# Joining small TensorE runs: scores and values of two head pairs together, retention's values turned, the compressed branch's first layer on four column groups

## The chip, the cores and the metric

One core of a Trainium2 chip. The time is what the device takes for one launch, in microseconds (us), on inputs of a fixed seed. The numbers are medians of several runs; a profile is one execution, recorded by the hardware profiler. Lower is better. The engines are TensorE (PE, with its weight loads shown apart as PEld), VectorE (DVE), ScalarE (ACT), GpSimd (POOL) and SyncE (SP), which issues the transfers.

## What is computed

Two transformer blocks over 256 tokens of width 1024, batch 1. The first block mixes four attention branches, each weighted by a gate of the normed input, then runs a gated feed-forward layer with a width-3 convolution. The second mixes retention with differential attention, attends to a memory of 256 tokens, and ends in another feed-forward layer. Cut to what the change touches:

```python
# first block
o_a = nsa_mixer(...)        # 4 heads of 64: compressed + selected + windowed attention, added with gates
o_b = dilated_mixer(...)    # 3 groups of 2 heads of 64, merged by a joint softmax
o_c = forgetting_mixer(...) # 4 heads (64, and 2 more columns for the decay)
o_d = mla_mixer(...)        # 4 heads (64 + 32 rotary)
merged = sum(sigmoid(h @ w_merge_gate[i]) * (o_i @ w_branch[i]))
# in nsa_mixer: 15 overlapping blocks of 32 tokens x 64, flattened to 2048
def compress(kv, w1, w2):
    blocks = (blocks + cmp_pos).reshape(b, n_cmp, 2048)
    return gelu(blocks @ w1) @ w2       # w1 2048 x 128, for keys and for values
# second block
scores = einsum('bhncd,bhnjd->bhncj', q, k) * decay        # retention, 8 heads of 64
o_ret = scores @ v
a = softmax(q0 k0) - lam * softmax(q1 k1)                  # difference, 4 heads, 2 maps of 64
o_diff = a @ v                                             # v 128 wide
```

## The kernel before

**Products.** The large matrices are streamed in panels. `W` (L479) loads a panel of fp32 weights into a `raw` slot, ACT rounds it to a shorter format into `hi`, DVE writes the remainder into `lo`; `mm3` (L492) then adds three products (high by high, high by low, low by high). `lin` (L597) does this for a panel of 512 columns and two halves of 128 tokens. The attention products work on plain fp32: one such product is two records in the trace.

**Planner.** Nothing is issued as it is written. `Plan.add` collects each operation with its operands; `Plan.trial` simulates the engines with the costs that `_Op` gives each operation, with limited slots for each class of buffer (8 PSUM banks `PS`; in SBUF 3 `raw`, 8 `hi`, 8 `lo`, 6 `k4`, 2 `g4`, 10 `k2`, 9 `k1` and others, L423), and picks by priority; a buffer is taken only if enough are free. `hurry` changes priorities where PE would wait, 120 trials are made, and the shortest is issued in its order of starts. So every change of cost or of buffers plans the whole order anew. `glue` (L160) makes all PE operations inside it one item of the plan, issued without a break. `AN.copy` and `AN.scale` go to DVE or ACT, whichever the plan finds free.

**Attention.** A head pair is worked together: `scores` (L645) issues four products, two heads by two halves of queries, glued; for 64-row heads the two heads stand on rows 0 to 63 and 64 to 127 of the array. DVE adds the bias and takes the minimum, `expo` (ACT) the exponential with its sum, `transP` (L666) transposes three 128 x 128 blocks on PE and copies them back, and `values` (L675) issues four products, glued, whose 64 held columns write partitions 0 to 63 and 64 to 127 of one bank. `attend` (L684) strings these together for one pair and one set of keys. The plain branches d and c call it twice each, branch a four times (two pairs, selected and windowed); branch b (L1165 to L1188) calls `scores` three times, then `values` three times.

**The compressed branch** (L1065 to L1121). The input is split into `hi` and `lo` pieces of 30 columns side by side (`blk`), the four panels of `w1` go through `W`, and 32 products of 256 columns, 60 or 30 columns held, are added in one bank of 60 partitions; `fold` adds the two halves and turns the result.

**Second block** (L1453 to L1499). Retention: for each of four pairs a glued run of score products, DVE multiplies by the decay, then three products per head with 128 columns of scores held and the 64 columns of a head's values moved, into two banks of 128 tokens x 512. The difference heads call `scores` once each.

Of the kernel before, what the change touches and what calls it, by code (L numbers as in the profile page):

```python
# [16 lines left out]
OP = mybir.AluOpType  # L17
# [3 lines left out]
class Plan:  # L21
# [137 lines left out]
    @contextmanager  # L159
    def glue(self):  # L160

        self.gluing = True
        yield
        self.gluing, self.glued = False, None

    def trial(self, prio):
# [29 lines left out]
        while done < len(ops):  # L196
# [15 lines left out]
            for e, hp in heaps.items():  # L212
# [3 lines left out]
                while hp:  # L216
# [5 lines left out]
                    ok = True  # L222
                    for nm in o.own:
                        if nm in place:
                            continue
                        c = self.cls[nm]
                        need = 1 if order[c][ptr[c]] == nm else 1 + (99 if o.dma else self.reserve.get(c, 99))
# [122 lines left out]
class _Op:  # L350
    def __init__(self, plan, n, eng, go, name, outs, ins, k):
# [8 lines left out]
        elif eng == "PE":  # L360
            n_ = size if name == "matmul" else 128
            if name == "transpose":
# [55 lines left out]
def emit(ctx, tc, nc, T, out, dbg):  # L418
# [226 lines left out]
    def scores(qk, bias, mn, at):  # L645

        ps = [psS([128, 384]) for _ in qk]
        ss = [sb([128, 384], "k2", name="s") for _ in qk]  # L650
        plan.hold = list(ss)
        with plan.glue():
            for tt in (1, 0):
                for p, (q, k) in zip(ps, qk):
                    PE.matmul(p[:, COLS[tt]], q[:, tt * 128:tt * 128 + 128], k[:, :128 * (tt + 1)], start=True, stop=True)
        for tt in (1, 0):
            for u, (p, s) in enumerate(zip(ps, ss)):
                c = at(tt, u)
                V.tensor_tensor_reduce(s[:, COLS[tt]], p[:, COLS[tt]], bias[u][tt], 1.0, 3e38, op0=OP.add, op1=OP.min,
                                       accum_out=mn[:, c:c + 1])  # L660
        return ss
# [13 lines left out]
    def values(po, pts, vs, first, last):  # L675

        blocks = ((0, slice(0, 256), slice(0, 256)), (1, slice(128, 256), slice(256, 384)))
        with plan.glue():
            for n, (j, c, w) in enumerate(blocks if first else blocks[::-1]):
                for u in range(2):  # L680
                    PE.matmul(po[64 * u:64 * u + 64, c], vs[u][j], pts[u][:, w], start=first and n == 0,
                              stop=last and n == 1, skip_group_check=first and last)

    def attend(po, qk, bias, vs, gain=None, first=True, last=True):  # L684

        mn, den, rec = small(4), small(4), small(4)
        ss = scores(qk, bias, mn, lambda tt, u: 2 * tt + u)
        for tt in (1, 0):
            for u in range(2):
                c = slice(2 * tt + u, 2 * tt + u + 1)  # L690
                expo(ss[u], tt, mn[:, c], den[:, c])
        V.reciprocal(rec, den)
        if gain is not None:
            for tt in range(2):
                V.tensor_mul(rec[:, 2 * tt:2 * tt + 2], rec[:, 2 * tt:2 * tt + 2], gain(tt))
        for u in range(2):
            for tt in (1, 0):
                AN.scale(ss[u][:, COLS[tt]], ss[u][:, COLS[tt]], rec[:, 2 * tt + u:2 * tt + u + 1])
        pts = [transP(s) for s in ss]
        values(po, pts, vs, first, last)  # L700
# [17 lines left out]
def mats1(E):  # L718
# [229 lines left out]
    def plain(q, k, v, kd, key):  # L948

        oT = heads(key, 2)  # L950
        for p in range(2):
            hs = (2 * p, 2 * p + 1)
            po = psS([128, 256])
            attend(po, [(q[:kd, h], k[:kd, h]) for h in hs], [(cm(0), cm(1))] * 2,
                   [[v[j][:, h, :] for j in range(2)] for h in hs])
            outT(oT, p, po)
# [36 lines left out]
    aqT = sb([128, 2, 256], "k4", name="aqT")  # L993
# [68 lines left out]

    gate(0, "d")

    posT = sb([128, 16], "sm", name="posT")  # L1065
    G.dma_start(posT, T["posT"])
    w2 = sb([128, 2, 64], "k1", name="w2")
    G.dma_start(w2, T["w2"])
    blk = sb([128, 16, 60], "k8", F32R, name="blk")
    for kv in range(2):  # L1070
        t = sb([128, 16, 15], "k1", name="blkf")
        for par in range(2):
            base = akT[par * 64:(par + 1) * 64, kv, par:par + 1]
            src = bass.AP(tensor=base.tensor, offset=base.offset, ap=[list(base.ap[0]), [2, 16], [16, 15]])
            V.tensor_add(t[par * 64:(par + 1) * 64], src,
                         posT[par * 64:(par + 1) * 64, :, None].to_broadcast([64, 16, 15]))
        hh = blk[:, :, 15 * kv:15 * kv + 15]
        S.copy(hh, t)
        V.tensor_sub(blk[:, :, 30 + 15 * kv:45 + 15 * kv], t, f(hh))
# [11 lines left out]
    hn = sb([60, 256], "k1", name="h1n")  # L1091
    V.tensor_copy(hn, hp)
    fold = sb([60, 30], "k1", name="fold")
    V.tensor_add(fold, ident[:60, :30], ident[:60, 30:60])
    ht = psS([128, 64])
    for kv in range(2):
        PE.matmul(ht[:, 32 * kv:32 * kv + 30], hn[:, 128 * kv:128 * kv + 128], fold, start=True, stop=True)
    h1 = bass.AP(tensor=ht.tensor, offset=ht.offset, ap=[list(ht.ap[0]), [47, 2], [1, 15]])
    hs = sb([128, 3, 2, 15], "k1", name="gelu")
# [5 lines left out]
    w2k = sb([128, 2, 64], "k1", name="w2k")  # L1105
    V.tensor_copy(w2k, w2[:, 0, None, :].to_broadcast([128, 2, 64]))
    hv = sb([128, 4, 32], "k1", name="hv")
    V.memset(hv, 0.0)
    V.tensor_copy(hv[:, :, :15], hs[:, 0, 1, None, :].to_broadcast([128, 4, 15]))
    kc = sb([128, 2, 16], "k1", name="kc")  # L1110
# [42 lines left out]
    for pr in range(2):  # L1153
        po = psS([128, 256])
        for b in range(2):
            attend(po, [(aqT[64 * u:64 * u + 64, pr], akT[64 * u:64 * u + 64, 2 + b]) for u in range(2)],
                   [(tb(2 * pr + u, 0), tb(2 * pr + u, 1)) for u in range(2)],
                   [[av[j][:, b * 64:(b + 1) * 64] for j in range(2)]] * 2,
                   lambda tt: gts[tt][:, 2 * pr:2 * pr + 2, 1 + b], b == 0, False)
# [6 lines left out]
    ss = [scores([(bq[64 * j:64 * j + 64, gi], bk[64 * j:64 * j + 64, gi]) for j in range(2)],  # L1166
                 [(tb(4 + 2 * gi + j, 0), tb(4 + 2 * gi + j, 1)) for j in range(2)], mn,
                 lambda tt, j: 6 * tt + 3 * j + gi) for gi in range(3)]
# [591 lines left out]
```

## Time and profile before

| | |
|---|---|
| median of 3 runs | 871.64 us (871.44 to 871.86) |
| the profiled execution | 872.01 us |
| its span, first to last instruction | 870.2 us |
| PE busy | 858.7 us (99%), 4453 records of products |
| DVE busy | 663.0 us (76%) |
| ACT busy | 479.5 us (55%) |
| granted TensorE clock, mean | 0.997 |

A product's shown length contains the way through the array, so that neighbours overlap; what a product costs in a stream is the distance from its start to the next one's. "128\*64 128x256" in a row is held rows by held columns, then the written shape. The chip time of the profiled execution is 1.8 us above its span.

### The profile page before, as it was taken

Reading aid. Unit: us, or ns where it says so; the run is one execution under the profiler, and the core shown is the slowest. Engines: PE = TensorE matmul, PEld = TensorE weight load, DVE = VectorE, ACT = ScalarE, POOL = GpSimd, SP = SyncE. Lnnn points to the kernel's source line nnn. Section 1 sums busy time; section 2 is a strip of 40 time slices with the busy share of each in tenths; the row PEclk is TensorE's granted clock in tenths of the full one; section 3 lists DMA queues with packets and bytes.
Section 4 is the critical chain, followed back from the end, with each engine's and each line's share of the span. In section 5 each row is a group of like instructions: output and inputs, shape, how many; then the busy total and the mean of one; then the engine's idle time right before and its main releaser. Section 6 shows DMA issues by size and latency. Waiting matters only on the chain.

```text
span 870.2 us, 12251 instructions
## 1 busy us (share of the span) xinstructions
PE 858.7 (99%) x4453; PEld 719.8 (83%) x4453; DVE 663.0 (76%) x1201; ACT 479.5 (55%) x810; POOL 45.3 (5%) x58
## 2 busy tenths in 40 slices
PE   8999999999999999999999999999999999999998
PEld 7789877778887888888878887888888888888886
DVE  6986766775778999898988677968775687776663
ACT  5775564764555766655654357645644545544440
POOL 2100000000001000000010111201100000000000
PEclk9999999999999999999999999999999999999999
DMA  7657745466447666666536564454643566666641
GB/s 225 207 191 217 218 148 164 160 198 213 144 148 241 195 212 211 204 195 192 193 122 198 167 194 149 143 169 145 208 131 97 187 200 216 215 182 185 198 141 49
DMA packets 45200, 156.07 MB, mean 179 GB/s; under 512 B 5142, under 2 KB 6984, under 8 KB 45012
## 3 DMA queue, kind: packets, MB, share of 16 engines
q1 hardware_dynamic: 44228, 153.09, 56.1%
q0 software_dynamic: 896, 2.19, 0.8%
q8 instruction: 35, 0.57, 0.3%
q14 instruction: 25, 0.20, 0.1%
q10 hardware_dynamic: 16, 0.00, 0.0%
HBM read 154.21 MB, written 1.06 MB: 178 GB/s over the span
## 4 chain that ended last, share of the span: by engine, by line
PE 89%; DVE 5%; issue 2%; ACT 1%; DMA 1%; POOL 1%; DVEq 0%; POOLq 0%; ACTq 0%
PE bank L102 89%; DVE k L102 2%; DVE lo L102 1%; DVE x L102 1%; POOL sm L102 1%; DMA raw<-in_fdn 1%; DMA raw<-in_fupn 1%; ACT x L102 0%; DVE sm L102 0%; ACT junk L102 0%; ACT k L102 0%; ACT hi L102 0%; ACT k L112 0%; DVEq L1756 0%; ACT sm L102 0%
## 5 line engine op out<-in xcount | busy, mean ns | idle before, releaser
L102 PE MATMUL bank<-hi,x 128*128 128x512 f32 (+3 forms) x1556 | 494.3, 392 | 2.2 <-DVE x L102 1.4
L102 DVE TENSOR_TENSOR lo<-raw,hi 128x1024 fp32r<-128x1024 f32 (+3 forms) x280 | 334.7, 1203 | 79.5 <-ACT hi L102 77.9
L102 ACT CAST hi<-raw 128x1024 fp32r<-128x1024 f32 (+3 forms) x280 | 288.7, 1036 | 140.2 <-PE bank L102 57.9
L102 PEld LDWEIGHTS bank<-hi,x 128*128 128x128 f32 (+1 forms) x1556 | 288.5, 188 | 57.6 <-ACT hi L102 2.5
L102 PE MATMUL bank<-lo,x 128*128 128x512 f32 (+3 forms) x786 | 305.7, 391 | 2.7 <-DVE lo L102 2.2
L102 PEld LDWEIGHTS bank<-lo,x 128*128 128x128 f32 (+1 forms) x786 | 146.6, 187 | 33.0 <-DVE lo L102 4.5
L102 PE MATMUL bank<-x,hi 128*128 128x512 f32 x656 | 167.9, 392 | 0.0
L102 PEld LDWEIGHTS bank<-x,hi 128*128 128x128 f32 x656 | 119.2, 189 | 21.3
L102 PEld LDWEIGHTS bank<-x,lo 128*128 128x128 f32 x656 | 89.7, 190 | 6.5
L102 PE MATMUL bank<-x,lo 128*128 128x256 f32 x656 | 91.8, 282 | 0.0
L112 ACT COPY k<-bank 128x256 f32<-128x256 f32 (+3 forms) x78 | 31.1, 409 | 56.8 <-PE bank L102 52.3
L102 POOL TENSOR_TENSOR sm<-sm,nhalf 128x1 f32<-128x1 f32 (+3 forms) x36 | 35.8, 997 | 492.8 <-DVE sm L102 492.8
L102 PE MATMUL bank<-ident,k 128*128 128x128 f32 (+3 forms) x347 | 53.3, 275 | 1.0 <-DVE k L102 0.7
L102 PEld LDWEIGHTS bank<-ident,k 128*128 128x128 f32 (+3 forms) x347 | 41.5, 138 | 13.8 <-DVE k L102 4.7
L102 DVE TENSOR_TENSOR x<-bank,x 128x512 fp32r<-128x512 f32 (+4 forms) x62 | 36.2, 606 | 20.4 <-PE bank L102 19.4
L102 PE MATMUL bank<-k,k 64*128 64x256 f32 (+12 forms) x364 | 49.9, 327 | 0.7 <-ACT k L112 0.6
L102 PEld LDWEIGHTS bank<-k,k 64*128 64x128 f32 (+4 forms) x364 | 38.7, 176 | 11.5 <-issue 4.9
L102 DVE COPY k<-bank 128x256 f32<-128x256 f32 (+7 forms) x60 | 28.1, 473 | 22.3 <-PE bank L102 22.0
L102 DVE TENSOR_TENSOR k<-k,bank 128x256 f32<-128x256 f32 (+1 forms) x78 | 32.5, 418 | 8.2 <-ACT k L112 7.5
L102 ACT ACTIVATE k<-bank,sm 128x256 f32<-128x256 f32 (+1 forms) x38 | 20.0, 554 | 28.4 <-PE bank L102 17.4
L102 DVE SCALAR_TENSOR_TENSOR k<-k,k,k 128x255 f32<-128x255 f32 x72 | 34.3, 479 | 1.5 <-ACT k L102 0.7
L102 ACT ACTIVATE k<-k,sm 128x128 f32<-128x128 f32 (+1 forms) x60 | 26.6, 446 | 7.5 <-DVE sm L102 7.4
(121 smaller groups left out, 439.4 us busy)
## 6 DMA issues: line engine op xcount, KB each, us to landing
raw<-in_wi SPq DMA_DIRECT2D x42, 512.0 KB, 4.4
raw<-in_up SPq DMA_DIRECT2D x40, 512.0 KB, 4.1
raw<-in_fup SPq DMA_DIRECT2D x36, 512.0 KB, 4.3
raw<-in_wg SPq DMA_DIRECT2D x32, 512.0 KB, 4.3
raw<-in_fdn SPq DMA_DIRECT2D x22, 512.0 KB, 4.5
raw<-in_dn SPq DMA_DIRECT2D x22, 512.0 KB, 4.6
raw<-in_xkv SPq DMA_DIRECT2D x16, 512.0 KB, 4.3
raw<-in_wo SPq DMA_DIRECT2D x8, 512.0 KB, 4.4
```

The costliest lines, as they stand in the source:

```text
L102: op = _Op(self, n, eng, lambda: getattr(target, name)(*map(self.place, a), **{x: self.place(y) for x, y in k.items()}), name, outs, ins, k)
L112: alt = _Op(self, n, e2, lambda: getattr(t2, n2)(*map(self.place, a2), **k2), n2, outs, ins, k2)
```

## The change

- `scores`, `values` and `attend` take a list of jobs. The products of all jobs in a call stand in one glued run; the steps between are as before, job by job. Branches c and d pass both head pairs, branch a the selected and the windowed attention of a pair, branch b two groups and then one to `scores`, all three to `values`. The difference heads go two by two.
- Retention's scores go two pairs a run. Its values are issued by `values`: the 64 columns of a head's values are held and up to 256 columns of scores moved, which gives the outputs turned round (head columns by tokens); a copy and two transposes for each pair bring them into the same two output banks.
- The first compressed layer takes plain fp32 weights in two `g4` slots and an unsplit input (one `k2` tile): for each of 16 steps and for keys and values one product, 15 columns held and 128 moved, on one of four groups of 32 columns. It is issued in two glued runs of 16 products. A small product with `fold` adds the groups, after four copies.
- `aqT` goes from class `k4` to `k2`; several small tiles of the compressed branch share a tile.
- The planner: a glued item costs 300 ns more; small fp32 products inside a glued item cost half (64 rows or columns) or a quarter (15 columns) of before; an item that takes several buffers needs that many free.

The core of the diff:

```diff
+        self.glued.cost += extra
...
+                        k = taken[c] = taken.get(c, 0) + 1
+                        need = k if order[c][ptr[c]] in o.own else k + (99 if o.dma else self.reserve.get(c, 99))
...
+            elif plan.gluing and m == 15:
+                self.cost = n_ / 2.4 + 2.0
+            elif plan.gluing and (m == 64 or p == 64):
+                self.cost = n_ * 2 / 2.4 + 2.0
...
+    def scores(jobs):
...
+        ps = [[psS([128, 384]) for _ in j[0]] for j in jobs]
+        ss = [[sb([128, 384], "k2", name="s") for _ in j[0]] for j in jobs]
+        plan.hold = [x for y in ss for x in y]
         with plan.glue():
+            for j, pj in zip(jobs, ps):
+                for tt in (1, 0):
+                    for p, (q, k) in zip(pj, j[0]):
+                        PE.matmul(p[:, COLS[tt]], q[:, tt * 128:tt * 128 + 128], k[:, :128 * (tt + 1)], start=True, stop=True)
+        for (qk, bias, mn, at), pj, sj in zip(jobs, ps, ss):
...
+    def values(jobs):
...
-            for n, (j, c, w) in enumerate(blocks if first else blocks[::-1]):
+            for po, pts, vs, first, last in jobs:
+                for n, (j, c, w) in enumerate(blocks if first else blocks[::-1]):
+                    for u in range(2):
+                        PE.matmul(po[64 * u:64 * u + 64, c], vs[u][j], pts[u][:, w], start=first and n == 0,
+                                  stop=last and n == 1, skip_group_check=first and last)
+
+    def attend(jobs):
...
+        mds = [(small(4), small(4)) for _ in jobs]
+        sss = scores([(j[1], j[2], md[0], lambda tt, u: 2 * tt + u) for j, md in zip(jobs, mds)])
+        vals = []
...
+            vals.append((po, [transP(s) for s in ss], vs, first, last))
+        values(vals)
...
+        attend([(pos[p], [(q[:kd, h], k[:kd, h]) for h in (2 * p, 2 * p + 1)], [(cm(0), cm(1))] * 2,
+                 [[v[j][:, h, :] for j in range(2)] for h in (2 * p, 2 * p + 1)], None, True, True) for p in range(2)])
...
-    aqT = sb([128, 2, 256], "k4", name="aqT")
+    aqT = sb([128, 2, 256], "k2", name="aqT")
...
+    blk = sb([128, 2, 16, 15], "k2", name="blk")
...
+    hp = psS([128, 128])
+    for cc in ((0, 1), (2, 3)):
+        ws = [sb([128, 1024], "g4", name="w1") for c in cc]
+        for c, w in zip(cc, ws):
+            plan.bulk = True
+            nc.sync.dma_start(w, T["w1"][c])
+            plan.bulk = False
+        with plan.glue():
+            for c, w in zip(cc, ws):
+                for i in range(4):
+                    for kv in range(2):
+                        r = 32 * (2 * (i % 2) + kv)
+                        PE.matmul(hp[r:r + 15], blk[:, kv, 4 * c + i], w[:, i * 256 + kv * 128:i * 256 + kv * 128 + 128],
+                                  start=c == 0 and i < 2, stop=c == 3 and i > 1)
...
-    hp = psS([60, 256])
-    for c in range(4):
-        hi, lo = W(T["w1"][c], 1024)
-        for i in range(4):
-            k = 4 * c + i
-            w = slice(i * 256, (i + 1) * 256)
-            if k == 15:
-                PE.matmul(hp[:30], blk[:, k, :30], lo[:, w], start=False, stop=False)
-            PE.matmul(hp, blk[:, k, :], hi[:, w], start=k == 0, stop=k == 15)
-            if k < 15:
-                PE.matmul(hp[:30], blk[:, k, :30], lo[:, w], start=False, stop=False)
...
+    for r in (0, 32, 64, 96):
+        AN.copy(hn[r:r + 15], hp[r:r + 15])
+    h1 = psS([128, 2, 15])
+    PE.matmul(h1.rearrange("p a c -> p (a c)"), hn, p1[:, 218:248], start=True, stop=True)
...
+        attend([(po, [(aqT[64 * u:64 * u + 64, pr], akT[64 * u:64 * u + 64, 2 + b]) for u in range(2)],
+                 [(tb(2 * pr + u, 0), tb(2 * pr + u, 1)) for u in range(2)],
+                 [[av[j][:, b * 64:(b + 1) * 64] for j in range(2)]] * 2,
+                 lambda tt, b=b: gts[tt][:, 2 * pr:2 * pr + 2, 1 + b], b == 0, False) for b in range(2)])
...
+    ss = scores([job(0), job(1)]) + scores([job(2)])
...
+        vals.append((po, pts, [[bv[kt][:, 2 * gi + j, :] for kt in range(2)] for j in range(2)], gi == 0, gi == 2))
+    values(vals)
...
-            PE.matmul(po[0][:, h, :], d[:, :128], rv[0][:, h, :], start=True, stop=True)
-            PE.matmul(po[1][:, h, :], d[:, 128:256], rv[0][:, h, :], start=True, stop=False)
-            PE.matmul(po[1][:, h, :], d[:, 256:], rv[1][:, h, :], start=False, stop=True)
+            for i, p in enumerate(pp):
+                for j in range(2):
+                    for u in range(2):
+                        r = slice(64 * u, 64 * u + 64)
+                        PE.matmul(ps[i][u][:, 256 * j:256 + 128 * j], rkT[r, p, 128 * j:128 * j + 128], rqT[r, p, 128 * j:],
+                                  start=True, stop=True)
...
+        pT = [psS([128, 256]) for _ in pp]
+        values([(pT[i], ds[i], [[rv[j][:, 2 * p + u, :] for j in range(2)] for u in range(2)], True, True)
+                for i, p in enumerate(pp)])
+        for i, p in enumerate(pp):
+            oT = sb([128, 256], "k1", name="rT")
+            AN.copy(oT, pT[i])
+            for tt in range(2):
+                PE.transpose(po[tt][:, 2 * p:2 * p + 2, :].rearrange("p h d -> p (h d)"), oT[:, tt * 128:tt * 128 + 128], ident)
...
+    for hp in ((0, 1), (2, 3)):
+        mds = [(small(4), small(4)) for _ in hp]
+        sss = scores([([(dqT[64 * b:64 * b + 64, h], dkT[64 * b:64 * b + 64, h]) for b in range(2)], [(cm(0), cm(1))] * 2,
+                       mds[i][0], lambda tt, b: 2 * b + tt) for i, h in enumerate(hp)])
```

## Rows read from the trace of the kernel before

**Rows 1.** The page's engine table: busy us, share of the span, instructions.
```profile
PE 858.7 (99%) x4453; PEld 719.8 (83%) x4453; DVE 663.0 (76%) x1201; ACT 479.5 (55%) x810; POOL 45.3 (5%) x58
```
**Rows 2.** Slices of 20 us: length, busy us of each engine, clock, DMA.
```profile
0.00:20.00 20.00, 16.93 (x75) 14.76 (x76) 13.84 (x50) 11.83 (x27) 4.61 (x11) 0.91 0.71 227
...
860.00:880.00 20.00, 6.26 (x28) 4.86 (x26) 2.83 (x5) 0.00 (x0) 0.00 (x0) 0.92 0.14 53
```
**Rows 3.** PE in order of time near 122 us: start, length, products, idle before.
```profile
121.92 0.39 PE L102 MATMUL bank<-hi,x 128*128 128x512 f32 x1
...
122.37 0.39 PE L102 MATMUL bank<-hi,x 128*128 128x512 f32 x1
122.69 0.92 PE L102 MATMUL bank<-k,k 64*128 64x256 f32 x8
...
123.88 0.40 PE L102 MATMUL bank<-lo,x 128*128 128x512 f32 x1
```
**Rows 4.** The same near 534 us: three calls of the difference heads.
```profile
533.66 0.62 PE L102 MATMUL bank<-hi,x 128*128 128x512 f32 x2
534.21 2.23 PE L102 MATMUL bank<-k,k 64*128 64x256 f32 x24
...
536.71 0.40 PE L102 MATMUL bank<-hi,x 128*128 128x512 f32 x1
```
**Rows 5.** The same near 136 and 148 us: one and two calls of values.
```profile
135.84 0.87 PE L102 MATMUL bank<-k,k 128*64 128x256 f32 x8
136.64 0.74 PE L102 MATMUL bank<-hi,x 128*128 128x512 f32 x2
...
147.83 1.52 PE L102 MATMUL bank<-k,k 128*64 128x256 f32 x16
149.28 0.50 PE L102 MATMUL bank<-hi,x 128*128 128x512 f32 x1
149.61 0.40 PE L102 MATMUL bank<-lo,x 128*128 128x512 f32 x1
```
**Rows 6.** The same: the first 64-row scores, and one ahead of values.
```profile
101.42 0.92 PE L102 MATMUL bank<-k,k 64*128 64x256 f32 x8
...
138.01 1.72 PE L102 MATMUL bank<-k,k 64*128 64x256 f32 x16
```
**Rows 7.** The same: the first and the last values of the first block.
```profile
49.15 1.41 PE L102 MATMUL bank<-k,k 66*128 66x128 f32 x12
...
179.22 1.52 PE L102 MATMUL bank<-k,k 128*64 128x128 f32 x16
```
**Rows 8.** PE by form, 488.3 to 490.7 us: busy us, mean ns, idle.
```profile
L102 PE MATMUL bank<-k,k 128*128 128x64 f32 x22 | 2.6, 272 | 0.0
```
**Rows 9.** PE in order of time near 543 us: transposes.
```profile
543.03 1.36 PE L102 MATMUL bank<-ident,k 128*128 128x128 f32 x11
```
**Rows 10.** The same from 154 to 161 us: the compressed branch's first layer.
```profile
154.44 0.30 PE L102 MATMUL bank<-hi,x 128*60 128x256 f32 x1 [0.82 <-DVE x L102]
...
158.11 0.75 PE L102 MATMUL bank<-hi,x 128*60 128x256 f32 x3
158.79 0.92 PE L102 MATMUL bank<-k,k 64*128 64x256 f32 x8
160.66 0.50 PE L102 MATMUL bank<-lo,x 128*128 128x512 f32 x1 [0.95 <-DVE lo L102]
```
**Rows 11.** DVE by form, 148 to 162 us.
```profile
L102 DVE TENSOR_TENSOR lo<-raw,hi 128x1024 fp32r<-128x1024 f32 x4 | 4.8, 1218 | 0.8 <-ACT hi L102 0.8
```
**Rows 12.** Slices of 5 us, columns as in rows 2.
```profile
150.00:155.00 5.00, 4.18 (x26) 3.17 (x25) 4.92 (x10) 3.25 (x5) 0.00 (x0) 1.00 0.36 105
155.00:160.00 5.00, 4.71 (x39) 3.95 (x37) 5.00 (x13) 1.05 (x1) 0.00 (x0) 1.00 0.39 104
```
**Rows 13.** One slice of 8 us beside the difference heads.
```profile
540.00:548.00 8.00, 6.57 (x47) 5.21 (x48) 7.89 (x26) 8.00 (x26) 0.60 (x1) 1.00 0.20 67
```
**Rows 14.** ACT in order of time near 540 us: one exponential.
```profile
540.10 0.49 ACT L102 ACTIVATE k<-k,sm 128x256 f32<-128x256 f32 x1
```

More of the change, by code (lines that the diff above doesn't have):

```diff
@@ L222, in trial @@
                     ok = True
+                    taken = {}
                     for nm in o.own:
@@ L684, in attend @@
[L684 to L688, printed above, removed]
-            for u in range(2):
[L690 to L700, printed above, removed]
+            for po, pts, vs, first, last in jobs:
[3 more added lines that the diff above has]
+                                  stop=last and n == 1, skip_group_check=first and last)
@@ new lines, in attend @@
+    def attend(jobs):
+        mds = [(small(4), small(4)) for _ in jobs]
+        sss = scores([(j[1], j[2], md[0], lambda tt, u: 2 * tt + u) for j, md in zip(jobs, mds)])
+        vals = []
+        for (po, qk, bias, vs, gain, first, last), (mn, den), ss in zip(jobs, mds, sss):
+            rec = small(4)
+            for tt in (1, 0):
+                for u in range(2):
+                    c = slice(2 * tt + u, 2 * tt + u + 1)
+                    expo(ss[u], tt, mn[:, c], den[:, c])
+            V.reciprocal(rec, den)
+            if gain is not None:
+                for tt in range(2):
+                    V.tensor_mul(rec[:, 2 * tt:2 * tt + 2], rec[:, 2 * tt:2 * tt + 2], gain(tt))
+            for u in range(2):
+                for tt in (1, 0):
+                    AN.scale(ss[u][:, COLS[tt]], ss[u][:, COLS[tt]], rec[:, 2 * tt + u:2 * tt + u + 1])
+            vals.append((po, [transP(s) for s in ss], vs, first, last))
+        values(vals)
@@ L1092, in mats1, with phisrc @@
[L1092 to L1099, printed above, removed]
+    blk = sb([128, 2, 16, 15], "k2", name="blk")
+    def phisrc(kv, par):
+        return akT[par * 64:(par + 1) * 64, kv, par:par + 1]
@@ new lines, in mats1 @@
+    w2, p1, p3 = (sb([128, 256], "k1", name=n) for n in ("p2", "p1", "p3"))
+    w2, w2k = w2[:, :128].rearrange("p (a d) -> p a d", a=2), w2[:, 128:].rearrange("p (a d) -> p a d", a=2)
+    G.dma_start(w2, T["w2"])
+    hn = p1[:, :128]
+    hs = p1[:, 128:218].rearrange("p (i a c) -> p i a c", i=3, a=2)
+    hv = p3[:, :128].rearrange("p (a c) -> p a c", a=4)
+    kc = p3[:, 128:160].rearrange("p (a c) -> p a c", a=2)
+    fold = p1[:, 218:248].rearrange("p (a c) -> p a c", a=2)
+    turn = ident.rearrange("p (a b c) -> p b a c", a=2, b=2)
@@ L1165, in mats1, with job @@
     mn, den = small(12), small(12)
[L1166 to L1168 removed]
+    def job(gi):
+        return ([(bq[64 * j:64 * j + 64, gi], bk[64 * j:64 * j + 64, gi]) for j in range(2)],
+                [(tb(4 + 2 * gi + j, 0), tb(4 + 2 * gi + j, 1)) for j in range(2)], mn,
+                lambda tt, j: 6 * tt + 3 * j + gi)
+    ss = scores([job(0), job(1)]) + scores([job(2)])
     mx, rec = small(4), small(4)
@@ L1186, in mats1 @@
             pts.append(transP(ss[gi][j]))
-        values(po, pts, [[bv[kt][:, 2 * gi + j, :] for kt in range(2)] for j in range(2)], gi == 0, gi == 2)
+        vals.append((po, pts, [[bv[kt][:, 2 * gi + j, :] for kt in range(2)] for j in range(2)], gi == 0, gi == 2))
+    values(vals)
     outT(oT, 0, po)
@@ L1349, in mats2 @@
     rsq, sumsq, split_T, gload, norm_T = g["rsq"], g["sumsq"], g["split_T"], g["gload"], g["norm_T"]
-    scores, expo, transP, recip, COLS = g["scores"], g["expo"], g["transP"], g["recip"], g["COLS"]
+    scores, values, expo, transP, recip, COLS = (g[n] for n in ("scores", "values", "expo", "transP", "recip", "COLS"))
     ident, xs, cm, ropeR, out = g["ident"], g["xs"], g["cm"], g["ropeR"], g["out"]
```

116 lines of the change are left out of this document (43 added, 73 removed).

## The prediction

> **What bounds the kernel now.** Read the engine table first [rows 1]: TensorE (PE) is busy for 858.7 of 870.2 us, so it stands for 11.5 us in all. The slices show where [rows 2]: 3.1 us in the first 20 us and 3.9 us in the last 10 (10.2 us of span, 6.3 of them busy). Some 4.5 us are left in between, and that is the most that better cover could ever give there. The rest of any gain must come out of PE's own work. I count that work from start to start, not by the busy column, in which neighbours overlap: a 512-column product is shown as lasting 0.39 us, but the one at 122.37 starts 0.45 us after the one two places ahead of it, so each takes 0.225 [rows 3].
>
> Now look at small products. One `scores` call on 64 rows is a run of 8 records (an fp32 product is recorded twice). A 512-column product starts at 122.37, the run at 122.69, and after one more product the next starts at 123.88 [rows 3]. From 122.37 to 123.88 is 1.51 us; less two products (0.45) the run took 1.06. Three calls that happen to stand together take, from 533.66 to 536.71, 3.05 us; less three products (0.68) that is 2.37 [rows 4]. So a further call costs (2.37 - 1.06) / 2 = 0.655 us, and entering and leaving a run 0.40 us, however long it is. The same for `values` [rows 5]: one call lasts 0.80 us to the next start, two together 1.45, so 0.65 for a call and 0.15 at its ends; the product behind the run takes 0.33 instead of 0.225, 0.10 more, and the one ahead of a run 0.09 more [rows 3]: 0.35 for entering and leaving. All this is PE time that the page calls busy, and the change merges runs.
>
> **The change, part by part.**
>
> *Scores.* The seven 64-row calls of the first block (four of branch a, three of b) stand in seven runs before, from 101.42 to 158.79 [rows 6, 10]; after, they are issued as four. Three entries and exits at 0.40 make 1.2 us. But one call stood right ahead of a `values` run (138.01, 16 records in 1.66 us to the next start [rows 6]), so part of an entry was saved already, and one stood right ahead of the compressed branch's products. I take 0.9; the ends are 0.4 and 1.2. In the second block the four retention and the four difference calls stood as three and one ([rows 4] has the three of difference), two runs each; after, two and two, also two runs: the work and the entries are the same, so nothing. Branches c and d have 66 and 96 rows, whose products stand among full-array ones; joining them moves no entry of this kind, and I take nothing.
>
> *Values.* Eleven calls stand in eight runs, from 49.69 (inside the first row) to 179.22 [rows 7]: branch d 2, c 1, a 3, b 2. After: 1, 1, 2, 1 = 5. Three times 0.35 make 1.1 us; the ends are 0.4, if neighbours that met by chance no longer do, and 1.8, if two more of the issued runs meet.
>
> *Retention's values.* Before, 24 fp32 products with 128 columns of decayed scores held and 64 columns of values moved, 48 records. 22 of them take 2.6 us, of which the last one's 0.27 is tail: 21 steps of 0.111 [rows 8], so 48 cost 5.3 us. After: four `values` calls in two runs, 4 x 0.65 + 2 x 0.35 = 3.3 us, and 8 transposes. 11 transposes took 1.36 us, less the same tail is 10 steps of 0.109 [rows 9]: 8 cost 0.9. Sum 4.2, a gain of 1.1 us. The four copies between fall to ACT or DVE; the products of the later `wi_2` panels, which need nothing of retention, can run beside them, so they cost nothing. Uncovered, the last copy and its two transposes would be late for the norm of the halves, below 1 us.
>
> *Compressed branch, first layer.* Before, 32 products of 256 columns: the first starts at 154.44, the 32nd at 158.11, 0.118 each, 3.8 us [rows 10], and about 0.3 for entering (they followed a run directly). After: 32 fp32 products with 15 columns held and 128 moved, 64 records, over four column groups, in two runs. A `values` call spends 0.65 us on two column groups with 2 x 256 + 2 x 128 columns in each: 0.108 per 128 columns. That is what a 128-column transpose alone costs [rows 9], so the second group is free there. If four groups overlap as two do, 16 quartets cost 16 x 0.108 = 1.7 us, and two entries 0.7: 2.4. If only pairs overlap, 3.5 + 0.7 = 4.2; one after another, 6.9 + 0.7 = 7.6. No row of before has four groups. I take 2.4, because where two groups are seen the second adds nothing, and keep 4.2 for the range. Gain 1.7 (bounds -0.1 and 2.0). The fold of the result becomes one small product in place of two; I take nothing.
>
> What four groups at once ask is 27 ns for each record, and no row shows such a pace: the `values` run issues 8 records in 0.65 us, 81 ns for each. If the issue of records set this pace and not the columns, 64 records would cost 5.2 us. [...]
>
> *Waits.* The same layer no longer splits its weights: four subtractions of 1.22 us on DVE go [rows 11], with four casts on ACT and the splitting of its input. They fell into the stretch where DVE was busy 4.92 and 5.00 of each 5 us [rows 12], and where PE stood 0.82 us for the split input and 0.95 us for a late `lo` panel [rows 10]. With some 5 us of DVE work gone most of that should go too; I take 1.0 of the 1.77. The weights now land in the two slots of the gains' class, so the second pair of transfers waits for the first run's products; SyncE issues in one order, and panels queued behind that wait come later. The split panels already in the eight `hi` and `lo` slots feed PE meanwhile; without that cover it would cost up to one transfer. Against the gain stands that a joined run needs four free banks and four tiles of scores at once, and that joined values wait for the later call's softmax. I take 0.5 us of new waits (bounds 0 and 2), since PE stood ahead of only a few of these runs before.
>
> *Sum.* 0.9 + 1.1 + 1.1 + 1.7 = 4.8 us of PE work, plus 1.0, less 0.5: 5.3 us. The profiled execution took 872.0 us (span 870.2), so 866.7. The median of the runs, 871.6, lies 0.4 below it: 866.3.
>
> **The rivals.** (1) New waits eat half. A joined retention run holds four of the eight banks, its turned values two and the outputs two: all eight, while panel products need banks too. In the first block, of the ten slots that hold scores, a joined call of branch a takes four, then four more for the transposed ones, and `aqT` now sits there as well. For it: from 540 to 548 us, beside the difference calls, PE stood 1.4 us with DVE and ACT full [rows 13], and there two calls are now joined. Against it: 4.5 us is all that PE stood between the ends. With 2.5 us more waiting: 868.8.
> (2) Four groups keep to the pace of a record seen here: 5.2 + 0.7 against 4.1 before, so this part loses 1.8 where I have it gain 1.7; 3.5 us worse, 869.8, about the bound of no change (0.2%, 1.7 us, is what a measurement of this kernel can tell).
> (3) Slower: the joined `values` of branches a and b have no cover. Each would then wait for one more call's softmax, four exponentials of at most 0.49 us on ACT [rows 14], up to 2.0 us, and some of DVE's share that can't overlap: 2.5 taken. It takes three such waits (7.5, against 4.8 saved) to pass the former time: 874.3. For it: DVE was full from 150 to 160 [rows 12]; against it: the gates' panels of three branches are still to be done then.
>
> **How the numbers follow.** Forecast, with about 0.5 us of new waits: 0.58. Rival 1: 0.20. Rival 2: 0.13. Rival 3: 0.06; something else without a gain 0.03. The likeliest time is 866.3. The lower end has all 1.8 us of waits gone, no new ones, and scores and values near their upper bounds: 864.2. The upper end takes in rival 1 and reaches rival 2: 869.9. Faster by over 0.2% (below 869.9): 0.58 + 0.20 + half of rival 2 = 0.85; within 0.2%, the other half and a little more: 0.08; slower: 0.07.
>
> **What would show it.** In the profile after: `scores` runs of 16 records some 1.5 us from start to next start; five `values` runs in the first block; 64 short records in two runs of about 0.9 us; no 64-column fp32 products but the two of the compressed values; PE's busy time down by about 5 us, and shorter waits between 150 and 165. It would be wrong if the short records start 60 ns apart or more on the mean, if PE waits for banks at 477 to 500 or for ACT and DVE near 540, or if the joined `values` show idle ahead of them.

## The result

The changed kernel takes 865.57 us (median of 4 runs, 864.47 to 866.16) where the kernel before takes 871.66 beside it: a ratio of 0.9925 (95% interval 0.9912 to 0.9937), 6.1 us faster. Forecast were 866.3, in a range of 864.2 to 869.9. The profiled execution of the changed kernel was its fastest, 864.47 us, 7.5 below the 872.0 of the one before; the shares below are shares of that 7.5.

The engine table of the page after, first the span (beside [rows 1]):

```profile
span 862.6 us, 12278 instructions
PE 852.5 (99%) x4475; PEld 714.0 (83%) x4475; DVE 657.8 (76%) x1197; ACT 476.5 (55%) x810; POOL 46.6 (5%) x58
```

PE is busy for 6.2 us less, and stands for 862.6 - 852.5 = 10.1 us in place of 11.5. So four fifths of the gain between these two executions are PE's own work, and the rest is waiting. Slices after, columns as in [rows 2]:

```profile
0.00:20.00 20.00, 16.76 (x75) 14.75 (x76) 13.83 (x51) 11.66 (x27) 4.61 (x11) 0.91 0.69 227
150.00:165.00 15.00, 15.00 (x80) 11.93 (x79) 10.21 (x15) 6.97 (x10) 0.00 (x0) 1.00 0.49 143
525.00:555.00 30.00, 28.70 (x170) 22.79 (x168) 27.34 (x81) 23.30 (x62) 6.23 (x7) 1.00 0.42 135
```

The first 20 us are nearly what they were. From 150 to 165 us, where PE stood most in the first block [rows 10, 12], it no longer stands at all. From 525 to 555 it still stands for 1.3 us. One wait is new: 0.60 us in two pieces ahead of the first block's first transposes of scores, where the kernel before has no idle time (the bracket: idle before, and who ended it):

```profile
49.66 0.41 PE L102 MATMUL bank<-ident,k 128*128 128x128 f32 x2 [0.43 <-DVE k L102]
50.24 0.66 PE L102 MATMUL bank<-ident,k 128*128 128x128 f32 x4 [0.17 <-ACT k L112]
```

PE in order of time, after: the first layer's first run, a joined scores call, and two runs with joined values (start us, us, engine line op out<-in, shapes, xcount).

```profile
103.17 1.07 PE L102 MATMUL bank<-g,k 128*15 128x128 f32 x32
104.16 0.50 PE L102 MATMUL bank<-hi,x 128*128 128x512 f32 x1
...
127.90 1.58 PE L102 MATMUL bank<-k,k 64*128 64x256 f32 x16
129.41 0.74 PE L102 MATMUL bank<-hi,x 128*128 128x512 f32 x2
...
139.67 3.66 PE L102 MATMUL bank<-k,k 128*64 128x256 f32 x34
143.26 0.50 PE L102 MATMUL bank<-lo,x 128*128 128x512 f32 x1
...
183.27 2.17 PE L102 MATMUL bank<-k,k 128*64 128x256 f32 x24
185.37 0.73 PE L102 MATMUL bank<-hi,x 128*128 128x512 f32 x2
```

A joined `scores` call of 16 records takes 1.51 us to the next start; 32 records of the first layer take 1.00 (0.998 between the unrounded starts); at 139.67 two calls of values (16 records), one product of another kind (2) and a joined call of scores (16) have met in one run of 34; three calls of `values` stand together at 183.27, 2.10 us for 24 records. None of these rows has idle time ahead of it. The first block's values stand in five runs, from 55.44, 70.14, 139.67, 153.18 and 183.27 us, as forecast. PE by form, after (x count, then busy us, mean ns, idle us):

```profile
L102 PE MATMUL bank<-k,k 64*128 64x256 f32 x60 | 9.8, 404 | 0.0
...
L102 PE MATMUL bank<-k,k 128*64 128x256 f32 x60 | 9.4, 391 | 0.0
...
L102 PE MATMUL bank<-g,k 128*15 128x128 f32 x64 | 2.1, 274 | 0.0
...
L102 PE MATMUL bank<-k,k 128*128 128x64 f32 x2 | 0.4, 288 | 0.0
```

The 64-column fp32 products of retention are gone but for the two of the compressed values, as forecast.

To see what each term was worth, I counted PE's products in both traces from start to next start, less the idle time shown ahead of a product, and summed by kind of product. The sums are 858.3 us before and 852.1 after.

| kind of product | before, us | after, us | gain | forecast |
|---|---|---|---|---|
| scores on 64 rows | 12.22 | 11.41 | 0.81 | 0.9 |
| values, with retention's old and turned ones and all transposes | 50.11 | 48.20 | 1.91 | 1.1 + 1.1 |
| first layer and its fold | 4.35 | 2.23 | 2.12 | 1.7 |
| products of 512 moved columns | 657.65 | 656.48 | 1.17 | in the rows above |

The second row is 8.36 + 5.66 + 36.09 before (values, 64-column products, transposes) and 10.81 + 0.22 + 37.17 after. All other products make 134.0 and 133.8. The last row holds the part of each entry and exit that falls on the neighbours (the product ahead of the run at 103.17 takes 0.33 us in place of 0.225, the one behind it 0.34), but its 1.17 us is not clear of the order: counted the same way it is 656.5 and 656.1 us in two other orders of the old work (experiments 1 and 2) and 656.6 in another order of the changed one (experiment 3). So are the transposes of the second row, 36.1 to 37.5 us in the three orders of the old work and 37.2 and 38.1 in two of the changed one. The rest of that row is steady, 13.7 to 14.4 us against 11.0, and with eight transposes at 0.109 us [rows 9] leaves a gain of 2.1. Where PE still waits, in order of time from 526 to 540 us after:

```profile
533.83 1.41 DVE L102 SCALAR_TENSOR_TENSOR k<-k,sm,g 128x512 f32<-128x512 f32 x2
534.49 0.60 POOL L102 DMA_DIRECT2D k<-in_mem  x1 [8.41 <-ACT hi L102]
534.63 1.32 PE L102 MATMUL bank<-ident,k 128*128 128x128 f32 x8 [0.59 <-DVE k L102]
...
536.40 0.50 PE L102 MATMUL bank<-hi,x 128*128 128x512 f32 x1 [0.45 <-ACT x L112]
```

PE waits for the memory's first tile to be normed, and the transfer of the second tile is issued only at 534.49, 19 us after the first one's. The plan issues it when a `k4` slot is free; that it was the slot it waited for is read from the program, since the row names ACT.

### The profile page after: what moved, and what is told of

Its sections match the earlier page's. It is cut to its first block, busy times and chain, and to the rows that moved or that the text cites. A ratio compares the mean times of both kernels' runs of the same rounds, so it can differ in the third digit from the quotient of the medians.

```text
span 862.6 us, 12278 instructions
## 1 busy us (share of the span) xinstructions
PE 852.5 (99%) x4475; PEld 714.0 (83%) x4475; DVE 657.8 (76%) x1197; ACT 476.5 (55%) x810; POOL 46.6 (5%) x58
## 4 chain that ended last, share of the span: by engine, by line
PE 92%; DVE 3%; ACT 2%; issue 1%; DMA 1%; POOL 1%; DVEq 0%; ACTq 0%; POOLq 0%; SPq 0%
PE bank L102 92%; DVE x L102 1%; DVE k L102 1%; DVE lo L102 1%; DMA raw<-in_fdn 1%; ACT hi L102 1%; POOL sm L102 1%; ACT k L102 0%; ACT x L102 0%; ACT k L112 0%; DVE sm L102 0%; ACT junk L102 0%; DVEq L1790 0%; ACT sm L102 0%; DVE nhalf L102 0%
## 5 line engine op out<-in xcount | busy, mean ns | idle before, releaser
L102 PE MATMUL bank<-hi,x 128*128 128x512 f32 (+2 forms) x1540 | 488.7, 393 | 1.5 <-ACT hi L102 0.9
L102 DVE TENSOR_TENSOR lo<-raw,hi 128x1024 fp32r<-128x1024 f32 (+3 forms) x276 | 329.7, 1204 | 72.1 <-ACT hi L102 70.5
L102 ACT CAST hi<-raw 128x1024 fp32r<-128x1024 f32 (+3 forms) x276 | 284.4, 1037 | 127.7 <-PE bank L102 58.9
L102 PEld LDWEIGHTS bank<-hi,x 128*128 128x128 f32 x1540 | 286.6, 188 | 56.1 <-issue 1.2
L102 PE MATMUL bank<-lo,x 128*128 128x512 f32 (+2 forms) x770 | 302.3, 393 | 1.8 <-DVE lo L102 1.3
L102 PEld LDWEIGHTS bank<-lo,x 128*128 128x128 f32 x770 | 144.9, 188 | 32.6 <-DVE lo L102 3.9
L112 ACT COPY k<-bank 128x256 f32<-128x256 f32 (+5 forms) x86 | 33.9, 409 | 61.7 <-PE bank L102 57.3
L102 PE MATMUL bank<-k,k 128*64 128x128 f32 (+11 forms) x344 | 44.3, 332 | 0.0
L102 PEld LDWEIGHTS bank<-k,k 64*128 64x128 f32 (+4 forms) x344 | 33.2, 170 | 9.8 <-issue 4.8
L102 ACT ACTIVATE k<-bank,nhalf 128x512 f32<-128x512 f32 (+2 forms) x24 | 15.4, 643 | 31.4 <-PE bank L102 31.4
```

What stands on the lines that cost most here:

```text
L102: op = _Op(self, n, eng, lambda: getattr(target, name)(*map(self.place, a), **{x: self.place(y) for x, y in k.items()}), name, outs, ins, k)
L112: alt = _Op(self, n, e2, lambda: getattr(t2, n2)(*map(self.place, a2), **k2), n2, outs, ins, k2)
```

## The experiments

Each ran beside the kernel before, whose medians were 871.68 us beside experiments 1 to 4, 871.93 beside 5 to 8 and 872.02 beside 9 and 10. A ratio is to it.

**1. Only the planner's edits.** They are the part of the change that touches every instruction's place, so a better order could have been the whole gain. The kernel before with these lines:

```diff
+        self.glued.cost += extra
...
+                        k = taken[c] = taken.get(c, 0) + 1
+            elif plan.gluing and (m == 64 or p == 64):
+                self.cost = n_ * 2 / 2.4 + 2.0
```

> The kernel before with the planner's edits alone (300 ns on a glued item, half costs for small fp32 products, several free buffers asked for at once); every product as before. Theory A (the gain is work taken out of PE): PE busy within 0.7 us of the 858.7 of before, time 871.6 give or take 1.0. Rival P (a better order from truer costs is what gained): 869 or less, with PE busy unchanged and PE's idle time down by 2 us or more.

872.62 us, ratio 1.0015 (1.0006 to 1.0024): nothing gained, 0.9 us lost. PE's busy time is 857.5 us, 1.2 below the kernel before and outside the 0.7 expected, and it stands for 13.2 us in place of 11.5. The longest waits are 2.25 us ahead of the transposes at 542.49, in a slice where before lost 1.6, and 1.16 us ahead of those at 48.77:

```profile
525.00:555.00 30.00, 27.74 (x162) 22.23 (x161) 24.36 (x74) 21.78 (x59) 3.37 (x4) 1.00 0.42 144
```

**2 and 3. Another order of both kernels.** The planner tries priorities with a random generator; another seed gives another order of the same work.

```diff
-random.Random(1)
+random.Random(2)
```

> The kernel before with another seed for the planner's 120 trials; nothing else. It measures how much a new order of the same work moves the time. Theory A: PE busy within 0.7 us of 858.7 and the time within 1.5 us of 871.6. Rival (luck of the order): more than 2 us away.

> The changed kernel with another seed for the planner's trials; nothing else. Theory A: PE busy within 0.7 us of the 852.5 of the changed kernel, time within 1.5 us of 865.6, so still 4 to 7.5 us below the kernel before. Rival (luck of the order): the time goes above 868.

Before with the other seed: 873.24 us, ratio 1.0017 (1.0008 to 1.0026). After with it: 865.37, ratio 0.9927 (0.9914 to 0.9941). An order is worth up to about 1.5 us (1.6 in the kernel before, 0.2 in the changed one); the gain is there in both. PE's busy time missed its bound both times: 860.2 and 854.1 us are 1.5 and 1.6 above the first order's, where 0.7 was allowed, and 873.24 lies 0.1 outside its own bound. So the same work in another order and execution moves PE's busy time by some 1.6 us, and the differences of 1.6 to 2.7 us in the experiments below carry that uncertainty. Sums from start to start over one kind of product are steadier: in both orders of the changed kernel the scores come to 11.41 us and the values on 64 columns to 10.81.

The kernel before in its other order also has the two waits of [rows 10] again, with DVE busy for 14.7 us from 150 to 165:

```profile
155.82 0.30 PE L102 MATMUL bank<-hi,x 128*60 128x256 f32 x1 [1.01 <-DVE x L102]
...
162.05 0.50 PE L102 MATMUL bank<-lo,x 128*128 128x512 f32 x1 [0.96 <-DVE lo L102]
```

**4. The old first layer in the changed kernel.**

```diff
-        ws = [sb([128, 1024], "g4", name="w1") for c in cc]
-                        PE.matmul(hp[r:r + 15], blk[:, kv, 4 * c + i], w[:, i * 256 + kv * 128:i * 256 + kv * 128 + 128],
+        hi, lo = W(T["w1"][c], 1024)
+            PE.matmul(hp, blk[:, k, :], hi[:, w], start=k == 0, stop=k == 15)
```

> The changed kernel with the compressed branch's first layer as before (weights and input split, 32 products of 256 columns, the old fold), all else as changed. Theory A: PE busy up by 1.7 to 2.2 us (3.8 + 0.3 for 2.4, and a fold of four records for two), waits up by 0.5 to 1.5: 868.0 to 869.2. Rival W (the layer's worth is the DVE and ACT work that it drops): PE busy up by less than 1, idle up by 2 or more.

867.15 us, ratio 0.9949 (0.9937 to 0.9962), so the layer is worth some 2 us (1.6 by the medians, 2.1 by the ratios), less than expected: the time lies below 868.0 to 869.2, and the waits did not grow. Rival W is not borne out. PE is busy for 855.2 us, 2.7 more than after: from start to start 1.76 in the layer's products and 0.32 in the fold, which I had taken at nothing; the rest is spread. DVE has its four subtractions again, but the waits of [rows 10] do not come back. The layer now runs at 171 us, and PE is all but full in that slice; DVE, the third busy time, is not (12.29 of 15 us, against 4.92 and 5.00 of 5 in [rows 12]):

```profile
165.00:180.00 15.00, 14.93 (x82) 12.09 (x81) 12.29 (x21) 7.22 (x11) 0.00 (x0) 1.00 0.57 178
```

**5. Retention's old values in the changed kernel.**

```diff
-        values([(pT[i], ds[i], [[rv[j][:, 2 * p + u, :] for j in range(2)] for u in range(2)], True, True)
+                PE.matmul(po[0][:, h, :], d[:, :128], rv[0][:, h, :], start=True, stop=True)
+                PE.matmul(po[1][:, h, :], d[:, 128:256], rv[0][:, h, :], start=True, stop=False)
+                PE.matmul(po[1][:, h, :], d[:, 256:], rv[1][:, h, :], start=False, stop=True)
```

> The changed kernel with retention's values as before (24 products with 128 columns of scores held, 64 columns moved), its scores still two pairs a run. Theory A: PE busy up by 1.1 us (5.3 for 4.2), time 866.7 give or take 0.8. Rival: the turned values, with their copies and transposes, cost as much as they save: PE busy within 0.4 of 852.5. Second rival: the eight banks that the turned form needs cost waits, so that the old form is no slower: 865.6 or less.

868.89 us, ratio 0.9963 (0.9951 to 0.9976): 3.3 us above the changed kernel's median, more than the 1.1 forecast. The spans of the two profiled executions lie 4.5 us apart: PE's busy time, 854.1, tells 1.6 of it, and 2.9 are standing, above all 2.07 us ahead of the same transposes of the memory:

```profile
537.34 1.32 PE L102 MATMUL bank<-ident,k 128*128 128x128 f32 x8 [2.07 <-DVE k L102]
```

By kind, from start to start, the old products take 4.71 us here, against 2.91 for the turned calls of the changed kernel and 0.9 for eight transposes at 0.109. That is 0.9 us, the neighbours' share not counted on either side: near the 1.1, and against both rivals, which expected no loss.

**6. Every joined call job by job.**

```diff
+        if len(jobs) > 1:
+            for j in jobs:
+                attend([j])
+            return
```

and the same in `scores` and `values`.

> The changed kernel with every call of scores and values issued job by job (each its own glued run), retention's values turned and the first layer in column groups as changed; retention's score products stay joined. Theory A: PE busy up by 2.0 to 2.7 us (0.9 for scores, 1.1 for values, up to 0.7 for retention's four value calls), less if single runs happen to meet, then 1.3 at least; time 867 to 868.3. Rival 1 (joining costs waits): PE busy up, idle down by the same, time within 0.7 of 865.6. Rival: entering and leaving a run is hidden, PE busy within 0.5.

867.26 us, ratio 0.9946 (0.9933 to 0.996). PE is busy for 855.1 us, 2.6 more than after; from start to start the products of 512 columns around the runs have 1.3 of it, scores and values 0.8 each. More came apart than the first block's calls: retention's values and the difference heads each stand in one run more than after. PE in order of time, a single call and its neighbours:

```profile
126.73 0.61 PE L102 MATMUL bank<-hi,x 128*128 128x512 f32 x2
127.28 0.92 PE L102 MATMUL bank<-k,k 64*128 64x256 f32 x8
128.13 0.50 PE L102 MATMUL bank<-lo,x 128*128 128x512 f32 x1
128.46 0.63 PE L102 MATMUL bank<-hi,x 128*128 128x512 f32 x2
```

The single call takes 0.85 us to the next start and the joined pair above 1.51, so the second call costs 0.66; the product behind the run takes 0.33 in place of 0.225. These are the prices that were read from [rows 3, 4].

**7. Two column groups in place of four.**

```diff
-                        r = 32 * (2 * (i % 2) + kv)
+                        r = 32 * kv
```

> The changed kernel with the first layer's products on two of the four column groups (keys on one, values on the other), 64 records as before, in two runs. Theory A (columns set the pace and the groups overlap): the 64 records need 55 ns each instead of 27, 3.5 us for 1.75: PE busy up by 1.7, each run about 1.9 us instead of 1.0. Rival 2 (the issue of a record sets the pace): the same 27 ns each, nothing changes.

866.80 us, ratio 0.994 (0.9927 to 0.9954). The same 32 records, PE in order of time:

```profile
103.25 1.93 PE L102 MATMUL bank<-g,k 128*15 128x128 f32 x32
105.11 0.50 PE L102 MATMUL bank<-hi,x 128*128 128x512 f32 x1
```

They take 1.86 us to the next start, and with four groups 1.00. Both runs lost 0.86, 1.7 in all as forecast (PE's busy time, 854.7, is 2.2 up), so four groups do overlap.

**8. The first layer in four runs.**

```diff
-        with plan.glue():
-            for c, w in zip(cc, ws):
+        for c, w in zip(cc, ws):
+            with plan.glue():
```

> The changed kernel with the first layer in four glued runs of 8 products, one for each panel of weights, instead of two of 16. Theory A: two more entries and exits at 0.35: PE busy up by 0.7 us, each run about 0.56 us to the next start; less if two runs meet. Rival: the entry is a wait for the first weights of a form, hidden between runs of one kernel's own kind: PE busy within 0.2.

866.59 us, ratio 0.9938 (0.9925 to 0.9952), which does not part it from the changed kernel. The first two runs met again; of the other two one waits for its weights:

```profile
110.39 0.63 PE L102 MATMUL bank<-g,k 128*15 128x128 f32 x16 [0.89 <-DMA g<-in_w]
110.95 0.50 PE L102 MATMUL bank<-hi,x 128*128 128x512 f32 x1
```

A run of 16 records takes 0.56 us, one of 32 takes 1.00. So a record costs (0.998 - 0.560) / 16 = 27.4 ns, and 0.12 us are left per run for its own ends, the neighbours' share not counted. At each of the two split runs the product ahead takes some 0.1 us more (but for the one with the wait) and the product behind 0.11 more, so the entry is not hidden. PE's busy time, 853.6 us, can't decide it: it is 1.1 up where 0.7 was forecast for two more runs and only one was added.

**9. The memory in another slot.** The waits at 534 to 538 us go back to a `k4` slot. Here the memory is loaded to the two `g4` slots and normed in halves through `k2`; the two edits are not parted.

```diff
-        m = sb([128, 1024], "k4", name="mem")
+        m = sb([128, 1024], "g4", name="mem")
...
+        for i in range(2):
+            c = slice(i * 512, (i + 1) * 512)
+            xn = sb([128, 512], "k2", name="mn")
```

> The changed kernel with the second block's memory loaded into a slot of the gains' class instead of a k4 slot, and normed half by half through k2 tiles. In every trace so far PE's longest wait between its ends stands near 530 to 548 us (1.3 us in the changed kernel, 1.6 before, 2.3 to 2.4 in two of the experiments), ahead of the memory's transposes: DVE is full with the difference heads, and the memory is read only when a k4 slot comes free. Theory (the slot is what makes it late): the memory's transposes move ahead of the difference heads, the wait falls below 0.5 us, time 864.6 give or take 0.7. Rival (DVE and ACT are full there whatever comes first): the wait moves to another place between 500 and 560, the time stays within 0.6 of 865.6.

863.81 us, ratio 0.9911 (0.9895 to 0.9926): the lowest median of all, 1.8 us below the changed kernel's (1.2 by the ratios, whose intervals overlap). The transfers of the memory, by tile, of the changed kernel and of this one:

```profile
L102 POOL DMA_DIRECT2D k<-in_mem x2: 597/597/597, 515.4 to 534.5; - x2
```

```profile
L102 POOL DMA_DIRECT2D g<-in_mem x2: 572/575/578, 447.8 to 461.8; - x2
```

They are issued 68 and 73 us earlier, and PE no longer stands there:

```profile
525.00:555.00 30.00, 30.00 (x176) 24.74 (x175) 26.00 (x76) 21.02 (x54) 2.23 (x2) 1.00 0.35 107
```

In all it stands for 8.0 us (861.8 - 853.8) in place of 10.1, of which 1.3 are gone here and 1.1 in the first 20 us, which this edit does not touch. PE's busy time is 1.3 up, inside what an order moves.

**10. Experiment 5 with the other seed**, to see whether its wait belongs to retention's form or to that one order.

> The changed kernel with retention's values as before, as in the run of that name, with another seed for the planner's trials. That run lost 3.3 us where 1.1 was expected: 1.6 of it PE work, the rest a wait of 2.1 us at 537. Theory (that wait is this one order's): PE busy stays 1.3 to 1.9 above 852.5, the wait falls to about 1, time 867.0 to 867.9. Rival (the old form lengthens the way to the mixed heads and so makes the wait): the wait near 537 stays at 2 us or more, time 868.5 or above.

867.86 us, ratio 0.9956 (0.9943 to 0.9968), 2.5 above the changed kernel with the same seed (865.37). Its wait there is 1.51 us plus 0.36, and PE's busy time 854.9, so of the theory's three conditions only the time is met, and neither of the rival's. The profiled execution is the slowest of the five, 869.16 us, and a part of its loss is of another kind. Slices of 2 us, and PE in order of time:

```profile
537.00:539.00 2.00, 0.49 (x7) 0.30 (x6) 2.00 (x6) 2.00 (x9) 0.60 (x1) 1.00 0.02 4
539.00:541.00 2.00, 1.63 (x10) 1.06 (x9) 2.00 (x11) 2.00 (x5) 0.00 (x0) 0.81 0.75 250
541.00:543.00 2.00, 2.00 (x6) 1.63 (x5) 1.97 (x8) 1.73 (x8) 0.00 (x0) 0.50 0.03 12
543.00:545.00 2.00, 2.00 (x9) 1.55 (x9) 2.00 (x11) 1.97 (x8) 0.00 (x0) 0.84 0.00 0
```

```profile
541.42 0.63 PE L102 MATMUL bank<-hi,x 128*128 128x512 f32 x1
541.85 0.63 PE L102 MATMUL bank<-lo,x 128*128 128x512 f32 x1
542.27 1.06 PE L102 MATMUL bank<-hi,x 128*128 128x512 f32 x2
```

After the wait the granted clock falls to 0.50, and 512-column products start 0.43 us apart in place of 0.23; some seven of them, so about 1.5 us. The profiled execution is 1.3 us above the median and has the lowest mean clock of the five (0.996 against 0.998 to 1.0), so it is not shown that this fall is in the median. In the slice from 525 to 555 us the five orders with the old retention (before, experiments 1, 2, 5, 10) stand for 1.6, 2.3, 1.4, 3.3 and 1.9 us, the six with the turned one and the memory in `k4` (after, 3, 4, 6, 7, 8) for 0.8 to 1.3. That is an association in eleven profiles, of which experiments 7 and 8 nearly repeat the waits of the changed kernel; the nearest two, 1.4 and 1.3, hardly part, and the step that links them is not shown.

## Why the prediction was right, and where it wasn't

**The bound.** Right. PE's own work set the time, and its fall by 6.2 us makes most of the gain. With a part of that work restored (experiments 4 to 7) the medians lie 1.2 to 3.3 us above the changed kernel's; only experiment 5 clearly passes what an order alone is worth, and for the others the rows of the restored products carry the argument.

**Scores and values.** Right in mechanism and prices: 0.40 us for an entry and exit and 0.655 for a further call are found again in experiment 6. 2.0 us were forecast for the first block. The 2.6 of experiment 6 (1.7 us in the medians) hold more than that, since retention's values and the difference heads came apart as well, and are to be set against the 2.0 to 2.7 expected there. One saving the forecast took at nothing is seen: a retention run of scores and one of values met in 32 records from 478.88 us on. The difference heads stand in two runs of 16, as forecast.

**Retention's values.** The term was right: the old products cost 5.4 us (5.3 forecast) and the 8 transposes 1.1 (0.9), though an order moves the transposes by as much, and the kinds of product of experiment 5 give 0.9 us where 1.1 was forecast (PE's busy time rose by 1.6 there, and by 0.8 from experiment 3 to 10, the pair of the other seed). What the forecast lacked is that this stretch has standing that was longer with the old form in every order seen (1.4 to 3.3 us against 0.8 to 1.3). The medians lie 3.3 and 2.5 us up, beyond what the products alone explain.

**First layer.** The open question, whether four groups overlap, is answered: 27 ns for each record, as I took it. The layer and its fold gained 2.12 us by their own starts; the products ahead of and behind the two new runs take 0.41 us more than 0.225 each, so the new layer costs 2.4, as forecast, and 1.7 us are gained, as forecast. In that sum two terms were off and cancel, which is luck: I had given the old layer an entry of 0.3 and the fold nothing; by the starts in experiment 4 entering the old layer costs nearly nothing (from 170.17 to 170.76 two products of 512 columns and the layer's first take 0.59 us, 0.57 at 0.225 and 0.118 each), and the old fold 0.32 more than the new one. The old form brought back cost 2.7 in PE's busy time, of which the rest is spread.

**Waits.** The size was too small and the reason is not shown. The 1.77 us at 154 and 161 vanished whole, where 1.0 was forecast. That DVE lost the layer's subtractions is not enough to explain it: with them back, in the changed kernel's order, PE does not wait there (experiment 4). Nor were the waits one order's: the kernel before has them in its other order too, 1.96 us (experiment 2), and with the planner's edits alone 0.55 us is left ahead of the layer (experiment 1). In the orders that wait DVE is full around the layer, in experiment 4 it is not; which part of the change gave DVE room stays open. The 0.5 us of new waits came about as forecast in size, 0.60 us at 49.66 and 50.24, but experiment 1 stands for 1.16 us at the like place with no call joined by an edit, so joining is not shown to make them. From 525 to 555 us PE stands for 0.3 us less, which was not forecast. Between the ends that is some 3.0 us after, against 4.5. So waits gave 1.4 us by the profiles in place of a net 0.5, and PE's work 6.2 in place of 4.8; the two profiles lie 7.5 apart, the medians 6.1.

**Rival 1**, new waits eat half: no. At its own place, 540 to 548 us, nothing of it is seen, and PE does not stand at all from 477 to 500; the difference heads now start some 8 us earlier, and from 525 to 555 us PE stands for 1.3 us, against 1.6 before. **Rival 2**, four groups at the pace of a record seen before: refuted by the 27 ns, and by experiment 7, in which half the groups took 0.86 us longer a run. **Rival 3**, no cover for the joined values: refuted, the joined runs at 139.67 and 183.27 have no idle time ahead of them. That a better order alone made the gain, which I had not listed, is refuted by experiments 1 to 3: three orders of the old work have medians of 871.7 to 873.2 us, two of the changed one 865.4 and 865.6.

**Left open.** Why the wait for the memory is longer with retention's old form, and what took away the waits at the compressed branch's first layer. The parts brought back one by one cost 1.6, 3.3 and 1.7 us (experiments 4, 5, 6), 6.6 against a gain of 6.1; with some 1.5 us from an order to another this agrees, and can't be split finer.

## What to carry to other kernels

Where one engine is full, count its work from start to start: runs of small products cost an entry and an exit that the busy column hides, here 0.40 us for a run of scores and 0.35 for one of values. Joining them gained 0.81 us in the scores here, and the longer wait for the inputs was covered (no idle time ahead of the runs at 139.67 and 183.27); in another kernel, see first that its trace has other work to cover it. Before an edit is called the cause, run another order of the same work and the planner's edits alone, since waits come and go with the order: PE stood for 1.16 us at 48.77 in experiment 1 and not at all near there in the kernel before. And when a wait is named after an engine, look for the buffer behind it: with the memory in another slot, and normed in halves, 1.3 us of standing went, in one order, with no arithmetic changed.

## What the hardware showed beside that

- Two column groups give 32 records in 1.86 us, four in 1.00. Less the 0.12 us at the ends that is 54 and 27 ns for each record, so in either a group spends 0.109 us on each of its records of 128 moved columns, and the groups overlap fully. The moved columns alone do not set that time: [rows 8] has 0.111 us for a record that moves 64.
- The granted clock fell to 0.50 in experiment 10 after PE had stood 1.51 us, worked through eight transposes and stood 0.36 us, but stayed at 1.00 after 2.25 us ahead of transposes in experiment 1 and after 2.07 us, eight transposes and 0.29 us in experiment 5. So the length of the wait alone does not decide it in these rows. Experiment 5, the clock in the third figure from the end:

```profile
525.00:555.00 30.00, 26.74 (x163) 20.78 (x163) 26.31 (x81) 22.99 (x64) 3.19 (x5) 1.00 0.39 125
```

- In the first 20 us the granted clock differs between executions of nearly the same work, 0.91 after, where PE is busy for 16.76 us with 75 records, and 0.83 in experiment 3, where it is busy for 16.96 us with 73. The shown clock does not tell it all: experiment 9 shows 1.00 there, and PE is busy for 17.86 us with 73 records. Such differences are a part of what separates two executions: of the 1.3 us by which PE's busy time is up in experiment 9, 1.1 lie there. Experiments 3 and 9:

```profile
0.00:20.00 20.00, 16.96 (x73) 14.62 (x74) 13.61 (x51) 11.81 (x27) 4.61 (x11) 0.83 0.70 228
0.00:20.00 20.00, 17.86 (x73) 15.26 (x74) 13.71 (x51) 11.80 (x27) 4.62 (x11) 1.00 0.69 226
```
